# A hybrid encoder layer on one core: retention parts stored side by side, a written order for two more units of the projections, a new order at the retention's start, and unread products at the attention's end

## The chip, the core and the metric

The kernel runs on one core of a Trainium2 chip. The metric is the device time of one execution in microseconds (us). The kernel before took 1525.36 us, the median of three runs (1524.49 to 1526.89).

## The reference, cut to what matters

One layer, 1024 tokens of 1024 channels, all in float32:

```
h = RMSNorm(x); proj = h @ w_in                  # columns: aq ak av | rq rk rv rg
attn = dilated window attention(aq, ak, av)      # 8 heads of 64, three windows mixed by softmax of their lse
ret  = silu(rg) * GroupNorm(retention both ways) # 4 heads, rq/rk of 64, rv of 128
x += concat(attn, ret) @ w_out
x += memory cross attention(RMSNorm(x), RMSNorm(mem))   # 4 heads, 256 memory slots
x += top-1 group, then top-2 SwiGLU experts(RMSNorm(x)) # 32 experts
```

Retention is the chunk-wise form: in each chunk scores = (q k^T) * decay, y = scores v, and y += (decayed q) state, with state a sum of (decayed k)^T v over the other chunks, once forward and once backward.

## The kernel before, in words

**Split products.** Every float32 matrix product with two large operands is made as three products of rounded parts (`mm3`, lines 120 to 122): high x high, low x high and high x low. ScalarE makes a high part (`split`, line 112, or line 116 with a scale), and VectorE or GpSimd the low part (line 113 or 117) from the source and the high part.

**Stages, in us from the span's start.** Input projections 0 to 299; attention 299 to 443; retention with the first half of the out-projection 443 to about 538; the out-projection's second half to 588; memory keys to 645; memory queries and scores per block of 128 tokens to 798; memory output and routing to 935; 32 experts to 1507; the last scatter to 1523.

**What sets the order.** A planner orders the instructions of each engine and places the waits, except inside `tc.manual_schedule()`, where each engine and queue gets its instructions in the order in which the program is written. Written order holds before for the first four units of the projections, the attention loop, the retention, the last memory block and the experts. An engine takes its instructions in order: one that waits holds up all behind it.

**Input projections** (the loop over `s_`, 48 units: six blocks of 512 columns, c = 0 to 5, with 8 units each). A unit is 24 products of 128x512 into one of five "mm" banks (`proj` and `projT`). `W.split(c + 1, i)` makes the next block's weights (`wih`, line 116, and `wil`, line 117). In block c = 3 (`unit_rqk`) the units j = 0 to 3 are retention queries: `chain()` splits the result (tile `spr`, stored to `rT_s` high and low by two transfers), multiplies it by two decay tables (`qd`, line 452) and splits each (`spqd`, four transfers of 128 KB to `qd_s`, lines 368 and 369). Units j = 4 to 7 are keys: `chain()` also copies the result (`kf`, line 448), and `tail()`, one unit later, turns `kf` by four transposes (`tkd`, line 466), scales them (`kd`, line 472) and splits them into two tiles `kt`, stored to `kd_s`. All these split tiles share the tag "sp", which has two slots: a new one can be written when the store of the one two before it has landed. Block c = 4 (`unit_rv`) does the retention's values and stores `rvt` to `rv_s` by four transfers a unit, issued from SyncE's queue (SP).

**Attention's end.** `plan(n, f, place)` hangs work on the steps n = 0 to 82 of the loop; `planned(n, 0)`, `(n, 1)` and `(n, 2)` run it at three places in a step. At the steps from 73 on the scores are all made, and TensorE has the last weighted sums (`oB`), the retention's first key-value sums (`kv`), and the expansions of the final factors (`RA`, `RB`, line 961), which VectorE multiplies in (`tA`, `tB`, line 962).

**Retention's start.** `wo_part` (lines 1172 and 1174) splits a quarter of w_out into `woh` (ScalarE) and returns a function that makes the low part `wol` (VectorE). Before, the four high parts are made together and ahead of `ret_scores(Hs[0], 0)` and `(.., 1)`. `ret_scores` forms `rs` (line 1094) in one of two "sc" banks, and VectorE multiplies by the decay (`w`, line 1096); `ret_low` makes `wh` and `wl` (lines 1098 and 1104). In the loop over 16 steps i, the low parts `wol` come at i = 0, 1, 2 (2: two of them); the first out-projection products (`out_a`, lines 120 to 122 as `po<-woh,mx`) come from i = 2 on, and need `mx`, the split of the attention's result.

**Last memory block.** With u = 7 the products `vw` = values x w_mo (line 1831's banks) run between the block's scores; `put()` splits a result into `VW`, `Wm.split` makes `wmh` and `wml`, and `m_softmax(u, c)` is one piece: maximum (lines 1584, 1585), two exponentials with sums on ScalarE (line 1588), reciprocal and product (lines 1590, 1591).

**Experts.** Of each expert e: `gate_up` (products `p`), `x_T` (turning the next expert's gathered tokens, `xt`, line 1695, split into `x`), `h_T` (turning the activation, `ht`, line 1733), `h_split`, and the down products. `xt` and `ht` share the two banks of "tr". Ahead of the loop six small VectorE instructions (`nblk`, `nbi`, `nxf`, `nxi`, lines 2198 to 2203) count the blocks of overfull experts, for use behind the loop.

Of the kernel before, what the change touches and what calls it, by code (L numbers as in the profile page):

```python
# [20 lines left out]
P = 128  # L21
S = 1024
# [24 lines left out]
def kernel(  # L47
# [159 lines left out]
    rT_s = [dram([512, S], F32, f"rT_s{i}") for i in range(2)]  # L207
    qd_s = [dram([512, S], F32, f"qd_s{i}") for i in range(2)]
# [110 lines left out]
    with ExitStack() as c1:  # L319
# [51 lines left out]
        def parts(tag, name):  # L371
            t = st.tile([P, 4, 2, P], F32R, tag=tag, name=name).rearrange("p a i c -> p (a i c)")
            return [t[:, 512 * i:512 * i + 512] for i in range(2)]

# [3 lines left out]
        qw = col_weight(qnw, 1, "qw")  # L378
        kw = col_weight(knw, 1, "kw")
# [33 lines left out]
        def side_by_side(name):  # L413

            return st.tile([P, 4, 2, P], F32R, tag="sp", name=name)
# [20 lines left out]
        def unit_rqk(c, j):  # L436
# [6 lines left out]
            def chain():  # L443
                h, l = parts("sp", f"spr{f}{half}_")
                split(h, l, ps)
                store2([t[f * P:f * P + P, hs] for t in rT_s], h, l)
# [3 lines left out]
                for d in range(2):  # L450
# [3 lines left out]
                    h, l = parts("sp", f"spqd{f}{half}{d}_")  # L454
                    split(h, l, qd, pool)
# [24 lines left out]
        def unit_rv(c, u):  # L480
            ps = bank("mm", 5, f"prv{u}")

            def chain():
# [11 lines left out]
                for t in range(4):  # L495
                    nc.sync.dma_start(rv_s[:, 32 * r:32 * r + 32, 4 * half + t].rearrange("h p c -> p h c"),
                                      vt[32 * t:32 * t + 32])
# [123 lines left out]
        tail = None  # L621
        for s_ in range(48):
            c, j = divmod(s_, 8)
# [19 lines left out]
            if s_ == 10:  # L643
                log_decays()
            if s_ == 17:
                attn_consts()
# [8 lines left out]
            if s_ == 36:  # L655
                ret_consts()
# [42 lines left out]
    def load_qk(H):  # L699
# [3 lines left out]
        for i in range(2):  # L703
            nc.sync.dma_start(H.KS[64 * i:64 * i + 64].bitcast(F32), rT_s[i][256 + 64 * hd:256 + 64 * hd + 64, :])
            for j in range(2):
                nc.sync.dma_start(H.QQ[i][64 * j:64 * j + 64].bitcast(F32), rT_s[i][64 * hd:64 * hd + 64, :])
# [65 lines left out]
    with ch, ExitStack() as c2:  # L772
# [243 lines left out]
        for hp in range(4):  # L1016
# [19 lines left out]
            plan(n + (32 if hp < 3 else 22), lambda hp=hp: finish(pairs[hp]))  # L1036
        plan(74, lambda: chunk_sum(Hs[1], 2))
# [31 lines left out]
    with c4:  # L1069
# [153 lines left out]
        with tc.manual_schedule():  # L1223
# [147 lines left out]
    with ExitStack() as c5:  # L1371
# [52 lines left out]
        with ExitStack() as c7:  # L1424
# [153 lines left out]
            def m_softmax(u, c):  # L1578
                sp = SP_.pop((u, c))
                if c == 0:  # L1580
                    PR[u] = sb_.tile([P, 4, NMEM], F32, tag="prob", bufs=1, name=f"prob{u}")
                prob = PR[u]
                mx = sm().tile([P, 2], F32, tag="mmx", name=f"mmx{u}{c}")
                dve.tensor_reduce(mx, sp.rearrange("p (h m) -> p h m", h=2), axis=AX, op=OP.max)
                dve.tensor_scalar(mx, mx, -1.0, None, op0=OP.mult)
                den = sm().tile([P, 2], F32, tag="mden", name=f"mden{u}{c}")
                for h in range(2):
                    act.activation(prob[:, 2 * c + h], sp[:, 256 * h:256 * h + 256], AF.Exp, bias=mx[:, h:h + 1],
                                   accum_out=den[:, h:h + 1])
                dve.reciprocal(den, den)  # L1590
# [788 lines left out]
```

## Time and profile before

| | us |
|---|---|
| runs | 1524.49, 1526.89, 1525.36; median 1525.36 |
| profiled execution, whole time | 1525.24 |
| its span | 1523.4 |
| TensorE busy | 1469.8 (96%) |
| VectorE busy | 1143.5 (75%) |
| ScalarE busy | 887.4 (58%) |
| GpSimd busy | 234.5 (15%) |
| mean granted TensorE clock | 0.985 |

The profiled execution is 0.12 us under the median, with 1.84 us around its span. TensorE is busy nearly throughout, so the time is its work plus its few idle stretches, and its work takes twice as long where the granted clock is 0.50.

### The profile page before, as it was taken

What the parts mean: (1) busy time and instruction counts of PE and PEld (TensorE: products, weight loads), DVE (VectorE), ACT (ScalarE), POOL (GpSimd) and SP (SyncE); (2) the same over time, 40 slices, a digit from 0 to 9 for tenths busy, and PEclk for the clock granted to TensorE, in tenths of its full rate; (3) what the DMA queues carried; (4) which work ended last, traced back from release to release, by engine and by line L of the source; (5) the groups of instructions that cost most, each with busy time, mean ns of one, the idle gap of its engine ahead of it and who ended that gap; (6) DMA issues with size and microseconds to landing.
All of it is one profiled execution on the core that took longest, in us unless ns stands there. A gap on an engine that the chain in (4) does not pass through costs nothing. (4 is left out here: it accounts for less than half of the span.)

```text
span 1523.4 us, 22386 instructions
## 1 busy us (share of the span) xinstructions
PE 1469.8 (96%) x7722; PEld 1173.2 (77%) x7722; DVE 1143.5 (75%) x2557; ACT 887.4 (58%) x1493; POOL 234.5 (15%) x203
## 2 busy tenths in 40 slices
PE   8999989999999999999999998999999999999995
PEld 7788878798988877888878886777777777776663
DVE  8865355287766675987685668899898899888894
ACT  6431233297862243734352325888888888887783
POOL 0000134234410000000000003222232222221111
PEclk9999999999989999999999999999999999999998
DMA  8446775778569874730236747999999999999992
GB/s 304 111 125 193 203 238 161 207 208 253 183 200 281 315 286 138 244 119 29 74 112 220 263 153 258 357 349 363 367 375 366 362 367 367 368 362 362 365 383 82
DMA packets 121045, 383.64 MB, mean 252 GB/s; under 512 B 16288, under 2 KB 49312, under 8 KB 94432
## 3 DMA queue, kind: packets, MB, share of 16 engines
q1 hardware_dynamic: 112960, 361.32, 67.9%
q0 software_dynamic: 7968, 20.86, 5.4%
q8 instruction: 62, 1.02, 0.3%
q14 instruction: 55, 0.45, 0.1%
HBM read 318.81 MB, written 71.70 MB: 256 GB/s over the span
## 5 line engine op out<-in xcount | busy, mean ns | idle before, releaser
L120 PE MATMUL p<-eh,x 128*96 128x512 f32 x384 | 152.9, 398 | 0.2 <-ACT x L112 0.2
L122 PE MATMUL p<-el,x 128*96 128x512 f32 x384 | 151.5, 395 | 0.0
L121 PE MATMUL p<-eh,x 128*96 128x512 f32 x384 | 151.0, 393 | 0.1
L1685 POOL DMA_INDIRECT xg<-h_s,idx x32 | 79.1, 2472 | 282.8 <-PE xt L1695 276.1
L113 DVE TENSOR_TENSOR el<-ews,eh 128x1024 fp32r<-128x1024 f32 x86 | 100.7, 1219 | 14.1 <-ACT eh L112 14.1
L112 ACT ACTIVATE eh<-ews 128x1024 fp32r<-128x1024 f32 x86 | 87.3, 1054 | 19.3 <-DMA ews<-in_w_down_dram 9.6
L113 DVE TENSOR_TENSOR el<-ex,eh 128x1024 fp32r<-128x1024 f32 x76 | 89.3, 1219 | 5.5 <-ACT eh L112 5.0
L112 ACT ACTIVATE eh<-ex 128x1024 fp32r<-128x1024 f32 x76 | 77.8, 1055 | 9.8 <-PE p L121 6.5
L122 PEld LDWEIGHTS p<-el,x 128*96 128x96 f32 x384 | 62.1, 162 | 26.6
L121 PEld LDWEIGHTS p<-eh,x 128*96 128x96 f32 x384 | 62.2, 162 | 25.3 <-DVE x L113 0.4
L120 PEld LDWEIGHTS p<-eh,x 128*96 128x96 f32 x384 | 62.1, 162 | 24.6 <-ACT x L112 0.4
L1771 POOL DMA_INDIRECT out_dram<-yo,idx x32 | 50.0, 1562 | 170.0 <-ACT yo L1770 165.5
L113 DVE TENSOR_TENSOR el<-wraws,eh 128x1024 fp32r<-128x1024 f32 x60 | 70.3, 1219 | 3.4 <-ACT eh L112 3.3
L112 ACT ACTIVATE eh<-wraws 128x1024 fp32r<-128x1024 f32 x60 | 60.3, 1053 | 5.4 <-PE p L121 2.2
L1770 ACT ACTIVATE yo<-py,lists 96x512 f32<-96x512 f32 x64 | 43.2, 684 | 27.5 <-PE py L122 27.3
L113 DVE TENSOR_TENSOR ehl<-ex,ehl 128x1024 fp32r<-128x1024 f32 x46 | 54.0, 1215 | 0.0
L120 PE MATMUL po<-woh,mx 128*128 128x512 f32 x128 | 52.3, 408 | 1.8 <-DVE xr L1199 1.7
L120 PE MATMUL y<-VW,pT 128*128 128x512 f32 x128 | 53.0, 414 | 0.0
L113 DVE TENSOR_TENSOR ehl<-ews,ehl 128x1024 fp32r<-128x1024 f32 x44 | 51.8, 1217 | 1.5 <-ACT ehl L112 1.2
L120 PE MATMUL py<-ehl,hm 128*96 128x512 f32 x128 | 52.3, 408 | 0.0
L120 PE MATMUL mq<-wqh,hh 128*128 128x512 f32 x128 | 51.1, 401 | 1.0 <-ACT hh L112 1.0
L120 PE MATMUL pq<-wih,hTh 128*128 128x512 f32 x128 | 52.0, 406 | 0.0
(843 smaller groups left out, 4466.7 us busy)
## 6 DMA issues: line engine op xcount, KB each, us to landing
ews<-in_w_down_dram SPq DMA_DIRECT2D x30, 1024.0 KB, 14.3
ex<-in_w_gate_dram SPq DMA_DIRECT2D x25, 1024.0 KB, 13.6
wraws<-in_w_up_dram SPq DMA_DIRECT2D x23, 1024.0 KB, 13.0
ews<-in_w_gate_dram SPq DMA_DIRECT2D x20, 1024.0 KB, 10.5
ex<-in_w_up_dram SPq DMA_DIRECT2D x19, 1024.0 KB, 13.6
ews<-in_w_up_dram SPq DMA_DIRECT2D x15, 1024.0 KB, 11.8
ex<-in_w_down_dram SPq DMA_DIRECT2D x15, 1024.0 KB, 12.6
wi<-in_w_in_dram SPq DMA_DIRECT2D x11, 1024.0 KB, 6.2
```

The lines of the kernel that those rows point to most:

```text
L112: act.activation(hi, src, AF.Copy)
L113: (lo_engine or dve).tensor_tensor(lo, src, hi.bitcast(F32), OP.subtract)
L120: pe.matmul(ps, ah, bh, start=first, stop=False, **kw)
L121: pe.matmul(ps, al, bh, start=False, stop=False, **kw)
L122: pe.matmul(ps, ah, bl, start=False, stop=last, **kw)
L1685: pool.indirect_dma_start(out=self.xg[0:self.ns], out_offset=None, in_=h3_s, in_offset=bass.IndirectOffsetOnAxis(ap=self.ix, axis=0), boun ...
L1770: act.activation(yo[0:ns, 512 * c:512 * c + 512], self.py[c][0:ns], AF.Identity, scale=self.gate)
L1771: pool.indirect_dma_start(out=out, out_offset=bass.IndirectOffsetOnAxis(ap=self.ix, axis=0), in_=yo[0:ns], in_offset=None, bounds_check=S ...
```

## The change

In block c = 3 both parts of a split lie in one scratch tensor and go out in one transfer of 512 KB; the "sp" tag gets three slots; the units s_ = 24 to 39 are in written order, with the tail of unit 30 ahead of the next block's weight splits; the `rv_s` stores alternate between SP and GpSimd's queue; the retention's constants are made at unit 13 instead of 36. At the attention's end eight products of 128x128 are added whose result nobody reads. At the retention's start the scores come ahead of the first w_out split, the others are spread, and one "mm" bank is taken first. In the last memory block the softmax is in three pieces with a weight split between. Among the experts the first `h_T` uses a "y" bank, and the six small instructions come behind expert 1's `h_split`.

```diff
-    rT_s = [dram([512, S], F32, f"rT_s{i}") for i in range(2)]
-    qd_s = [dram([512, S], F32, f"qd_s{i}") for i in range(2)]
+    rT_s = dram([512, 2, S], F32, "rT_s")
+    qd_s = dram([512, 2, S], F32, "qd_s")
...
+        def both(name):
+            t = st.tile([P, 4, 2, P], F32R, tag="sp", bufs=3, name=name).rearrange("p a i c -> p (a i c)")
+            return t.rearrange("p (i t) -> p i t", i=2)
...
-                h, l = parts("sp", f"spr{f}{half}_")
-                split(h, l, ps)
-                store2([t[f * P:f * P + P, hs] for t in rT_s], h, l)
+                hl = both(f"spr{f}{half}_")
+                split(hl[:, 0], hl[:, 1], ps)
+                nc.sync.dma_start(rT_s[f * P:f * P + P, :, hs], hl.bitcast(F32))
...
-                    for j in range(2):
-                        hh = 2 * rp + j
-                        rows = slice(64 * j, 64 * j + 64)
-                        store2([t[P * hh + 64 * d:P * hh + 64 * d + 64, hs] for t in qd_s], h[rows], l[rows])
+                    hl = both(f"spqd{f}{half}{d}_")
+                    split(hl[:, 0], hl[:, 1], qd, pool)
+                    r0_ = 2 * P * rp + P * d
+                    nc.sync.dma_start(qd_s[r0_:r0_ + P, :, hs], hl.bitcast(F32))
...
+                    (nc.sync, pool)[t % 2].dma_start(rv_s[...], vt[32 * t:32 * t + 32])
...
+            if s_ == 24:
+                by_hand = c1.enter_context(ExitStack())
+                by_hand.enter_context(tc.manual_schedule())
+            if s_ == 40:
+                by_hand.close()
...
             p_()
+            if j == 7 and c == 3:
+                tail()
+                tail = None
             if j == 7 and c < 5:
                 for i in range(4):
                     W.split(c + 1, i)
...
+            if s_ == 13:
+                ret_consts()
-            if s_ == 36:
-                ret_consts()
...
     def load_qd(H):
         for i in range(2):
-            nc.sync.dma_start(H.qd[i].bitcast(F32), qd_s[i][H.hd * P:H.hd * P + P, :])
+            for d in range(2):
+                r0_ = 2 * P * (H.hd // 2) + P * d + 64 * (H.hd % 2)
+                nc.sync.dma_start(H.qd[i][64 * d:64 * d + 64].bitcast(F32), qd_s[r0_:r0_ + 64, i])
...
+        spare = []
+        plan(73, lambda: spare.append(bank("sc", 2, "spare")), 0)
+        for n in range(73, 77):
+            plan(n, lambda: busy_pe(spare[0], 2), 1)
...
-            wol = [wo_part(0, k // 2, k % 2, ro[:, k].rearrange("p (j f) -> p j f", j=2)) for k in range(4)]
+            wol = []
+            def wo_high(k):
+                wol.append(wo_part(0, k // 2, k % 2, ro[:, k].rearrange("p (j f) -> p j f", j=2)))
+            bank("mm", 1, "po_first")
             ret_scores(Hs[0], 0)
             ret_scores(Hs[0], 1)
+            wo_high(0)
             ret_low(Hs[0], 0)
...
                     wol[k]()
+                if i == 0:
+                    wo_high(1)
...
                     mix_part(0, 0, MX.pop(("r", 0)))
+                    wo_high(2)
+                    wo_high(3)
...
-                m_softmax(u, 0)
                 vw(4)
                 put()
+                held = Later(dve)
+                m_max(u, 0)
+                Wm.split(1, 0, held)
+                m_exp(u, 0)
+                held.go(1)
                 vw(5)
+                m_weights(u, 0)
                 put()
-                Wm.split(1, 0)
...
-                m_softmax(u, 1)
+                m_max(u, 1)
+                Wm.split(1, 1, held)
+                m_exp(u, 1)
+                held.go(1)
                 put()
-                Wm.split(1, 1)
+                m_weights(u, 1)
...
-            dve.tensor_scalar(nblk, nblk, float(P - 1), None, op0=OP.add)
-        ...
...
-                B[e].h_T()
+                B[e].h_T("y" if e == 0 else "tr")
                 B[e].h_split()
+                if e == 1:
+                    dve.tensor_scalar(nblk, nblk, float(P - 1), None, op0=OP.add)
+                ...
```

`busy_pe(ps, n)` makes n products of the 128x128 identity with itself; `Later` collects VectorE instructions and `held.go(1)` issues one.

## Rows read from the trace of the kernel before

**Rows 1.** The profile page: busy us (share of the span) and instructions of each engine.
```profile
PE 1469.8 (96%) x7722; PEld 1173.2 (77%) x7722; DVE 1143.5 (75%) x2557; ACT 887.4 (58%) x1493; POOL 234.5 (15%) x203
```

**Rows 2.** Waits of PE over the span: who waits, for whom, us in total, times, longest.
```profile
PE ht L1733 <- DVE x L113: 5.3, 5, 2.4
...
PE tkd L466 <- ACT kf L448: 2.6, 2, 2.4
PE vw L120 <- DVE VW L113: 2.6, 2, 1.3
...
PE prv L120 <- DVE qd L452: 1.4, 1, 1.4
...
PE po L122 <- DVE wol L1174: 1.1, 1, 1.1
```

**Rows 3.** Stretches of the span: start:end, length, busy us (and instructions) of PE, PEld, DVE, ACT and POOL, granted clock, DMA share, GB/s.
```profile
80.00:100.00 20.00, 20.00 (x95) 16.57 (x94) 13.58 (x51) 3.95 (x7) 0.00 (x0) 1.00 0.41 124
200.00:220.00 20.00, 16.23 (x74) 12.78 (x73) 14.77 (x27) 10.32 (x17) 5.85 (x9) 1.00 0.77 210
240.00:300.00 60.00, 60.00 (x264) 48.88 (x263) 17.44 (x28) 15.62 (x26) 18.10 (x34) 1.00 0.62 171
940.00:960.00 20.00, 17.59 (x85) 12.42 (x84) 18.68 (x25) 16.74 (x20) 2.48 (x2) 1.00 0.80 292
1000.00:1020.00 20.00, 20.00 (x95) 14.21 (x95) 18.23 (x20) 16.74 (x20) 5.84 (x3) 1.00 1.00 355
```

**Rows 4.** The chain of block c = 3: ScalarE in order of time (start, us, instruction, in brackets the idle time before it and what ended it).
```profile
185.46 0.60 ACT L112 ACTIVATE spr__1902<-prqk 128x512 fp32r<-128x512 f32 x1 [6.65 <-DMA qd_s<-spqd__1861]
...
194.43 0.60 ACT L112 ACTIVATE spr__1950<-prqk 128x512 fp32r<-128x512 f32 x1 [4.63 <-DMA qd_s<-spqd__1909]
...
200.00 2.74 ACT L116 ACTIVATE wih<-wi,mixw_t 128x512 fp32r<-128x512 f32 x4 [1.20 <-PE prqk L122]
...
216.09 0.60 ACT L448 ACTIVATE kf<-prqk 128x512 f32<-128x512 f32 x1 [1.37 <-DVE spr__2079 L113]
216.59 0.63 ACT L112 ACTIVATE kt<-kd 128x512 fp32r<-128x512 f32 x1
```

**Rows 5.** Transfers issued between 160 and 300 us, the group of 512 KB stores: tile, queue, count, KB each, median us from issue to landing.
```profile
kd_s<-kt SPq DMA_DIRECT2D x8, 512.0 KB, 3.0
```

**Rows 6.** The transposes of a key unit on PE, and VectorE's scaling of them, in order of time.
```profile
213.64 0.66 PE L466 MATMUL tkd<-ident,kf 128*128 128x128 f32 x4 [2.42 <-ACT kf L448]
...
214.33 1.13 DVE L472 TENSOR_SCALAR kd<-tkd,Gk 128x128 f32<-128x128 f32 x4 [1.38 <-PE tkd L466]
```

**Rows 7.** Stretches around idle time and clock changes, columns as in rows 3.
```profile
4.50:8.10 3.60, 0.01 (x1) 0.00 (x1) 2.14 (x11) 1.60 (x3) 0.00 (x0) 0.93 0.92 324
8.00:14.00 6.00, 5.90 (x17) 4.56 (x18) 5.41 (x13) 5.38 (x10) 0.00 (x0) 0.50 1.04 406
211.20:216.00 4.80, 2.38 (x14) 2.02 (x14) 3.22 (x9) 1.79 (x3) 0.00 (x0) 1.00 0.96 257
432.00:436.00 4.00, 3.29 (x26) 2.72 (x23) 2.29 (x7) 4.00 (x14) 0.00 (x0) 1.00 0.78 246
441.00:444.40 3.40, 3.09 (x21) 2.50 (x21) 1.41 (x3) 1.50 (x4) 0.00 (x0) 1.00 1.02 208
444.50:458.10 13.60, 12.40 (x49) 10.87 (x49) 9.91 (x17) 7.29 (x11) 0.57 (x1) 0.50 0.95 289
594.80:598.00 3.20, 3.20 (x9) 2.44 (x8) 2.76 (x8) 0.60 (x1) 0.00 (x0) 0.50 0.00 0
598.20:601.40 3.20, 3.20 (x16) 2.64 (x15) 0.00 (x0) 0.00 (x0) 0.00 (x0) 1.00 0.00 0
```

**Rows 8.** The retention's start in order of time, on ACT, DVE and PE.
```profile
448.36 3.88 ACT L1172 ACTIVATE woh<-ro 128x1024 fp32r<-128x1024 f32 x4
...
447.47 0.95 DVE L974 TENSOR_TENSOR tB<-tA,tB 128x768 f32<-128x768 f32 x1
...
454.01 0.68 DVE L1104 TENSOR_TENSOR wl<-w,wh 128x512 fp32r<-128x512 f32 x1
454.61 1.22 DVE L1174 TENSOR_TENSOR wol<-ro,woh 128x1024 fp32r<-128x1024 f32 x1
455.74 0.69 DVE L1096 SCALAR_TENSOR_TENSOR w<-rs,Dt_r 128x512 f32<-128x512 f32 x1
...
458.69 0.50 PE L121 MATMUL po<-woh,mx 128*128 128x512 f32 x1 [0.33 <-DVE mx L113]
```

**Rows 9.** The last memory block, DVE and PE in order of time.
```profile
779.20 0.17 DVE L1590 RECIPROCAL mden<-mden 128x2 f32<-128x2 f32 x1 [1.14 <-ACT prob L1588]
...
784.97 0.17 DVE L1590 RECIPROCAL mden<-mden 128x2 f32<-128x2 f32 x1 [1.15 <-ACT prob L1588]
...
786.52 0.50 PE L120 MATMUL vw<-wmh,vT 128*128 128x512 f32 x1 [1.30 <-DVE VW L113]
```

**Rows 10.** The first expert: DVE and PE in order of time.
```profile
941.34 0.17 DVE L2198 TENSOR_SCALAR nblk<-nblk 128x32 f32<-128x32 f32 x1
...
942.50 4.63 DVE L113 TENSOR_TENSOR el<-wraws,eh 128x1024 fp32r<-128x1024 f32 x4
...
949.92 1.01 DVE L113 TENSOR_TENSOR x<-xt,x 128x384 fp32r<-128x384 f32 x2
...
950.51 0.55 PE L1733 MATMUL ht<-ident,sg 96*128 96x96 f32 x4 [2.41 <-DVE x L113]
```

More of the change, by code (lines that the diff above doesn't have):

```diff
@@ L371, in parts @@
         def parts(tag, name):
-            t = st.tile([P, 4, 2, P], F32R, tag=tag, name=name).rearrange("p a i c -> p (a i c)")
+            t = st.tile([P, 4, 2, P], F32R, tag=tag, bufs=3, name=name).rearrange("p a i c -> p (a i c)")
             return [t[:, 512 * i:512 * i + 512] for i in range(2)]
+        def both(name):
+            t = st.tile([P, 4, 2, P], F32R, tag="sp", bufs=3, name=name).rearrange("p a i c -> p (a i c)")
+            return t.rearrange("p (i t) -> p i t", i=2)
         xts = {}
@@ L377 @@
         mixw_t = col_weight(mixw, KD, "mixw_t")
-        qw = col_weight(qnw, 1, "qw")
-        kw = col_weight(knw, 1, "kw")
+        qkw = consts.tile([P, 2], F32, name="qkw")
+        qw, kw = qkw[:, 0:1], qkw[:, 1:2]
+        nc.sync.dma_start(qw, qnw)
+        nc.sync.dma_start(kw, knw)
         W = Weights(w_in, whl, "wi", mixw_t)
@@ L413, in side_by_side @@
         def side_by_side(name):
-            return st.tile([P, 4, 2, P], F32R, tag="sp", name=name)
+            return st.tile([P, 4, 2, P], F32R, tag="sp", bufs=3, name=name)
         def unit_v(c, u):
@@ L495, in chain @@
                 for t in range(4):
-                    nc.sync.dma_start(rv_s[:, 32 * r:32 * r + 32, 4 * half + t].rearrange("h p c -> p h c"),
-                                      vt[32 * t:32 * t + 32])
+                    (nc.sync, pool)[t % 2].dma_start(rv_s[:, 32 * r:32 * r + 32, 4 * half + t].rearrange("h p c -> p h c"),
+                                                     vt[32 * t:32 * t + 32])
             return lambda: proj(ps, u, W.w[c]), chain, None
@@ L703, in load_qk @@
         for i in range(2):
-            nc.sync.dma_start(H.KS[64 * i:64 * i + 64].bitcast(F32), rT_s[i][256 + 64 * hd:256 + 64 * hd + 64, :])
+            nc.sync.dma_start(H.KS[64 * i:64 * i + 64].bitcast(F32), rT_s[256 + 64 * hd:256 + 64 * hd + 64, i])
             for j in range(2):
-                nc.sync.dma_start(H.QQ[i][64 * j:64 * j + 64].bitcast(F32), rT_s[i][64 * hd:64 * hd + 64, :])
+                nc.sync.dma_start(H.QQ[i][64 * j:64 * j + 64].bitcast(F32), rT_s[64 * hd:64 * hd + 64, i])
     def load_qd(H):
@@ L1576, in m_scores, with m_max, m_exp @@
                             dk == 0, dk == 1)
-            def m_softmax(u, c):
-                sp = SP_.pop((u, c))
+            def m_max(u, c):
                 if c == 0:
                     PR[u] = sb_.tile([P, 4, NMEM], F32, tag="prob", bufs=1, name=f"prob{u}")
-                prob = PR[u]
                 mx = sm().tile([P, 2], F32, tag="mmx", name=f"mmx{u}{c}")
-                dve.tensor_reduce(mx, sp.rearrange("p (h m) -> p h m", h=2), axis=AX, op=OP.max)
+                dve.tensor_reduce(mx, SP_[u, c].rearrange("p (h m) -> p h m", h=2), axis=AX, op=OP.max)
                 dve.tensor_scalar(mx, mx, -1.0, None, op0=OP.mult)
-                den = sm().tile([P, 2], F32, tag="mden", name=f"mden{u}{c}")
+                SP_["m", u, c] = mx
+            def m_exp(u, c):
+                sp, mx, prob = SP_.pop((u, c)), SP_.pop(("m", u, c)), PR[u]
+                den = SP_["d", u, c] = sm().tile([P, 2], F32, tag="mden", name=f"mden{u}{c}")
                 for h in range(2):
@@ L1594, in m_softmax @@
                     nc.sync.dma_start(prob_s[u * P:u * P + P, :], PR.pop(u).rearrange("p h m -> p (h m)"))
+            def m_softmax(u, c):
+                m_max(u, c)
+                m_exp(u, c)
+                m_weights(u, c)
             q_feat(0, tb)
@@ L1727, in swiglu, with h_T @@
                     dve.tensor_tensor(sv, sv, u, OP.mult)
-                def h_T(self):
+                def h_T(self, tag="tr"):
                     ns = self.ns
-                    self.hb = bank("tr", 2, f"ht{self.n}")
+                    self.hb = bank(tag, 2, f"ht{self.n}")
                     for i in range(4):
@@ L2197 @@
                 raws.free(B[0].raw(i), pool)
-            dve.tensor_scalar(nblk, nblk, float(P - 1), None, op0=OP.add)
-            dve.tensor_copy(nbi, nblk)
-            dve.tensor_scalar(nbi, nbi, 7, None, op0=OP.logical_shift_right)
-            dve.tensor_copy(nblk, nbi)
-            dve.tensor_reduce(nxf, nblk, axis=AX, op=OP.add)
-            dve.tensor_copy(nxi, nxf)
             for e in range(NEXP - 1):
@@ L2223 @@
                     B[e - 1].put()
-                B[e].h_T()
+                B[e].h_T("y" if e == 0 else "tr")
                 B[e].h_split()
+                if e == 1:
+                    dve.tensor_scalar(nblk, nblk, float(P - 1), None, op0=OP.add)
+                    dve.tensor_copy(nbi, nblk)
+                    dve.tensor_scalar(nbi, nbi, 7, None, op0=OP.logical_shift_right)
+                    dve.tensor_copy(nblk, nbi)
+                    dve.tensor_reduce(nxf, nblk, axis=AX, op=OP.add)
+                    dve.tensor_copy(nxi, nxf)
             e = NEXP - 1
```

5 lines of the change are left out of this document (3 added, 2 removed).

## The prediction

> **What bounds the kernel now.** I read the page first: TensorE is busy 96% of the span and no other engine comes near [rows 1]. The time is therefore TensorE's work at the granted clock, plus its idle stretches, and a change that adds or removes no large product can gain only idle time or half-rate time. So the next view was the list of TensorE's waits [rows 2]; the reader is to see that it is short, that no wait in it is over a few us in sum, and that most of its lines name an instruction that this change moves: the transposes of the retention keys, a value product behind `qd`, the products of values and w_mo, an out-projection product behind `wol`, and the experts' `ht`. Then came the stretches around these places [rows 3], for which engine is free to take what is moved in, and for the clock [rows 7], and at last each place in order of time, engine by engine.
>
> **Part A, the projections.** Before, TensorE idles 1.4 us ahead of a value product and 2.6 us ahead of two transposes [rows 2], 4.0 in all, which is the idle time of its stretch (16.23 busy of 20 [rows 3], the rest small). The row behind them is ScalarE's: a `spr` split waits 6.65 us for the store of an earlier `spqd` [rows 4]. The slots of "sp" make the chain late, and the transposes come when the chain lets them. After, three slots take the three tiles of a unit, and one 512 KB store replaces four issues. Such a store lands in 3.0 us by its nearest kin [rows 5]. A unit on TensorE is 24 products; 264 products take 60.00 us [rows 3], so 0.227 each and 5.5 a unit. A slot is held for the split (0.6 [rows 4]), the low part and the 3.0 of the store; that leaves 1.9 for a low part and its issue before the slots hold a unit up, so the chain just keeps pace. I take it that the 4.0 go.
>
> In written order something comes back. At unit 31 the tail of unit 30 stands between the products and the next weights. Its transposes are behind all 24 products of unit 31. From their start the first `kd` starts 0.69 later (214.33 against 213.64) and takes 1.13 [rows 6], the second takes as long again, to 2.9; `kt` takes 0.63, and the first `wih` 2.74/4 = 0.7 [rows 4], to 4.2. TensorE, whose transposes fill 0.66 [rows 6], has nothing else until then: 3.5 us idle. Before, this `wih` was made at 200.00 [rows 4], beside products, for the planner put it ahead. Bounds: 0, if a chain in hand lets ScalarE turn to the weights earlier, to 4.2. I take 3.5.
>
> Idle time has a second price. After 3.6 us without products (4.50 to 8.10) the granted clock was 0.50 in the stretch behind [rows 7]; around an idle 2.4 us (211.20 to 216.00) it stayed at 1.00 [rows 7]. 3.5 is nearest to the first, so I charge one half-rate stretch: 3.2 us of it do 9 products where 3.2 at full rate do 16 [rows 7], at half speed a loss of 1.6. Part A: -4.0 + 3.5 + 1.6 = **+1.1**, between -4.0 and +1.8.
>
> The rest of A I cost at nothing. The `rv_s` stores that go to GpSimd's queue fall where TensorE is busy 60.00 of 60 and GpSimd 18.10 [rows 3]; if GpSimd were late, its low parts of `rvt` would be, and nobody reads those before the retention. The constants moved to unit 13 are GpSimd work, two exponentials of ScalarE, in a stretch with GpSimd idle and TensorE full [rows 3]. `load_qd` issues four transfers instead of two a head, on SP, behind the loads of the attention's result, whose order is kept.
>
> **Part B and C, attention's end and retention's start.** From 444.50 to 458.10 the granted clock is 0.50, and TensorE is busy 12.40 of 13.60 [rows 7]: at full rate this is 6.2 us of work. The eight spare products lie in 432 to 441, where TensorE has some idle time (3.29 of 4.00 busy [rows 7]). A 128x128 transpose, the nearest row, costs 0.66/4 = 0.17 [rows 6], eight 1.3 at most; they fill gaps, so I cost them at 0. If the clock holds, VectorE bounds the stretch. Its instructions from `tB` on come in a line: `wl`, `wol` and `w` start at 454.01, 454.61 and 455.74 [rows 8], so 0.60 for a `wl` or `w` and 1.13 for a `wol`. `tB`'s add would end at about 447.75, when its earlier products run at full rate (448.42 before [rows 8]). Then come four `w`, three `wl`, two `wol` and 0.8 of `mx`, as written: 4.2 + 2.3 + 0.8 = 7.2, to 455.0. The new order is what lets them come without a gap, as 3.88 us of `woh` [rows 8] no longer stand ahead of the first `wh`. The mixed product of 458.69 [rows 8] comes at 455.0: -3.7. But 10.6 us with 6.2 of work leave TensorE 4.4 idle in pieces, the last of them long, so I charge one half-rate stretch here too: **-2.1**, between 0 and -3.7. The wait of 1.1 for `wol` [rows 2] stays: two `wol` still follow each other at i = 2, and their high parts now come later.
>
> A rule speaks against the spare products. What the rows show: in the 3.40 us before the fall TensorE was busy 3.09 [rows 7], with no idle stretch near those of part A. The Trainium skill, page "TensorE: Matmul & The Clock Gate", section "Why this matters for your kernels", has it that what costs the clock in the middle of a kernel are idle gaps of some length between bursts. By it the spare products would hold nothing, and B would be worth 0; the row differs from the rule, since the clock fell without such a gap. That case is the second rival.
>
> **Part D, last memory block.** TensorE waits 2.6 us, twice 1.3, for VectorE's `VW` [rows 2]. VectorE itself had waited 1.14 and 1.15 for the exponentials ahead of the reciprocals [rows 9]. The low part of `wm` (1.2 us, as other low parts of 1024 columns: 4.63/4 [rows 10]) now stands in these holes, and what follows moves up by the hole: 2.29 at most. I take **-2.3**; if only one wait goes, -1.0. ScalarE makes the high part ahead of the exponentials, while VectorE makes the maximum, so these are hardly later.
>
> **Part E, experts.** TensorE waits 2.41 for the first `ht`, whose bank `xt` held until `x` was split at 950.93 [rows 10]. In a "y" bank it waits for nothing but `sg`, and the six small instructions (941.34 to 942.50 [rows 10]) leave VectorE's line: everything behind them is 1.16 earlier. `x` then ends at 949.77 instead of 950.93, and the products that need its low part follow: **-1.5**, between -0.5 and -1.7. The six come behind expert 1, where TensorE is full; in such a stretch VectorE is busy 18.23 of 20 [rows 3], so they cost at most their 1.16 if that cover is gone.
>
> **Sum.** +1.1 - 2.1 - 2.3 - 1.5 = -4.8, against the profiled execution's 1525.24: 1520.4. That execution is 0.12 under the median of the runs, so the forecast stands for it as well. Less than about 0.2% (3 us) can't be told from no change.
>
> **Rivals.**
> 1. *The seam of unit 31 costs nothing.* The chain is so much in hand that weights and tail overlap, and no clock falls. For it: 4.0 idle are gone and VectorE has time. Against: one written order, and transposes behind the products. 1520.4 - 3.5 - 1.6 = 1515.3.
> 2. *Little comes through.* The clock falls at 444.5 all the same (spare products sit before 441, the fall comes later, and the clock fell with 3.09 of 3.40 busy [rows 7]); the new order alone gains about 1.1 there. And the experts are held by their weights: the DMA share is 1.00 [rows 3], so E's 1.5 is taken back. 1520.4 + 1.0 + 1.5 = 1522.9. Against the second half: the share is 0.80 at the place of E [rows 3], and a load starts when its slot is freed, so an earlier start is passed on.
> 3. *Slower: written order makes TensorE wait for the chain.* Before, the planner let the next block go on while the key chain was late: the value block's weights were made at 200.00, the `kf` of the second key unit at 216.09 [rows 4]. In written order every transpose, and the first `wih` behind the tail, waits for the chain. It decides when the lateness of eight units exceeds the 5.5 of slack that one unit gives: 0.7 a unit, a store of 3.7 us in place of 3.0. Price: at the pace of before, two query units' `spr` 9.0 apart (185.46 and 194.43 [rows 4]), 3.5 a unit are lost; four query units 14, less 5.5, is 8.5 and gives 1528.9; with key units as slow 14 more, 1542.9. I take the middle, 1536. Against it: 3.0 us for a store of this size [rows 5]; for it: written order gives no way around.
>
> **Chances.** Forecast, with its own range 1518 to 1522: 0.50. Rival 1: 0.15. Rival 2: 0.22, two thirds of it within 3 us of before. Rival 3: 0.13, nearly all of it slower. So faster by over 0.2%: 0.50 + 0.15 + 0.06 = 0.71; within: 0.17; slower: 0.12. The range holds forecast, rivals 1 and 2 and the near end of rival 3, 1515.0 to 1525.5; outside are most of rival 3 and some tails.
>
> **What would show it.** A right: no ScalarE wait of several us for `qd_s` or `rT_s`, `tkd` right behind products, and one idle stretch of about 3.5 us ahead of the first `prv`, with a clock of 0.50 behind it. B right: no 0.50 from 444.5. C right: the first mixed product about 11 us after `RB` starts. D: the two waits `vw` for `VW` gone. E: `ht`'s longest wait under 1 us. The prediction would be wrong if the transposes wait for `kf` again and again (rival 3), or if the gains are there until 935 and gone at the end (rival 2).

## The result and the profile after

The changed kernel took **1535.82 us**, the median of six runs (1532.10 to 1541.63), beside 1525.04 for the kernel before in the same runs (1521.34 to 1526.99). The ratio is 1.0066 with a 95% interval of 1.0047 to 1.0085: slower by some 10 us, where 1520.4 was forecast, in a range up to 1525.5. The profiled execution took 1537.01 with a span of 1535.2, 11.8 more than before.

The changed kernel's waits of PE, to be laid beside [rows 2]:

```profile
PE kv L120 <- DMA v_r<-rv_s: 4.2, 1, 4.2
...
PE prv L120 <- ACT wih L116: 3.6, 1, 3.6
...
PE oB L906 <- ACT phB L112: 3.3, 1, 3.3
PE ht L1776 <- DVE x L113: 3.2, 4, 1.1
...
PE vw L120 <- DVE VW L113: 1.2, 2, 0.7
```

Every wait that the prediction named for going is gone or shorter: the two for the late chain (`tkd`, `prv` behind `qd`) are not in the list, `vw` went from 2.6 to 1.2, and `ht` from 5.3 to 3.2 with a longest of 1.1. The predicted new one is there (`prv` behind `wih`, 3.6). But two large waits are there that the prediction doesn't know: 3.3 for `phB`, in the middle of the attention, and 4.2 for a load of `v_r`, in the retention. Around these places the change touches little but loads.

Stretches of the changed kernel around the three idle places and at the attention's end (columns as in [rows 3]; the DMA share is the mean busy share of the sixteen DMA engines, so 1.00 means all are busy):

```profile
205.20:208.90 3.70, 0.05 (x2) 0.01 (x1) 2.18 (x9) 1.93 (x4) 1.62 (x2) 0.81 0.42 166
208.90:214.30 5.40, 5.14 (x11) 3.65 (x12) 5.40 (x8) 4.72 (x8) 0.87 (x1) 0.50 0.48 194
365.60:369.00 3.40, 0.15 (x3) 0.03 (x1) 0.05 (x1) 1.16 (x3) 2.84 (x2) 0.84 1.03 230
369.00:378.20 9.20, 9.20 (x43) 9.20 (x44) 4.96 (x18) 6.05 (x20) 5.87 (x5) 0.50 0.29 94
443.00:453.20 10.20, 10.15 (x84) 9.61 (x85) 5.10 (x16) 3.17 (x8) 0.24 (x1) 1.00 1.03 303
453.20:456.60 3.40, 3.17 (x15) 2.88 (x15) 3.27 (x6) 1.58 (x3) 0.57 (x1) 0.51 1.03 258
...
463.50:466.90 3.40, 3.40 (x11) 2.83 (x10) 0.58 (x1) 0.00 (x0) 0.00 (x0) 0.50 1.07 246
509.00:514.00 5.00, 0.83 (x8) 0.65 (x7) 3.03 (x11) 1.32 (x3) 0.00 (x0) 1.00 1.03 215
514.70:518.10 3.40, 3.40 (x16) 3.24 (x16) 0.51 (x2) 0.00 (x0) 0.00 (x0) 0.50 1.02 354
```

Each idle stretch is followed by one at a granted clock of 0.50: 5.4 us of it behind the seam, 9.2 behind `phB` (all of it with PE fully busy, so about 4.6 us of work lost), 3.4 behind `v_r`. So each of the two unknown waits costs more than its idle time. At both the DMA share is 1.03 and the transfers bring 215 to 230 GB/s.

What stands behind `phB`, changed kernel in order of time on POOL, ACT and PE:

```profile
359.27 1.04 POOL L308 CAST QA<-QB 128x1024 fp32r<-128x1024 f32 x1 [17.48 <-PE sB L837]
...
365.48 2.33 POOL L988 TENSOR_TENSOR tB<-tA,tB 128x1024 f32<-128x1024 f32 x1
...
367.84 0.59 ACT L913 ACTIVATE tB<-oB 64x512 f32<-64x512 f32 x1 [6.19 <-POOL tB L988]
...
368.97 1.22 PE L906 MATMUL oB<-phB,vB 128*128 128x256 f32 x4 [3.25 <-ACT phB L112]
```

Read from the bottom: TensorE waits for ScalarE, which waited 6.19 us for GpSimd's `tB`; GpSimd ran without a pause from 359.27, and began only then, with the conversion of a loaded tile (`QB`). The engine named in its bracket (`PE sB`) had long been done; the experiments below show that it is the load. So one load that lands late, at 359, ends as an idle TensorE at 366.

To see where the 11.8 us arise, the trace of each kernel was cut at the same products (first or last start or end on TensorE), and the length of each piece taken, in us. "tail" is the changed kernel with the tail moved back (below), "half rows" and "half columns" are the kernel before with another load of `qd` (below):

```
piece (from .. to)                       before  changed  tail    half rows  half columns
projections, rqk to the end              140.13  141.97   135.62  141.04     141.05
attention, to its last score             115.43  120.79   119.83  118.76     115.11
to the last RB                            31.60   31.00    31.00   30.92      30.91
to the first mixed product                11.26    8.50     8.52   11.06      11.05
retention, to its last kv                 53.86   61.22    57.68   60.83      52.64
to the memory tokens' first transpose     78.73   80.81    80.79   80.34      78.73
to the first vw                          176.37  174.57   174.62  174.75     176.35
last memory block                         31.24   29.28    29.59   31.26      31.23
to the first expert's products           137.91  140.45   139.63  139.10     138.15
first expert's products to the last p    559.78  558.25   557.85  562.19     558.25
```

Against before, the changed kernel loses 1.8 in the projections, 5.4 in the attention, 7.4 in the retention, 2.1 behind it and 2.5 at the routing; it gains 0.6 and 2.8 at the retention's start, 1.8 ahead of `vw` (a half-rate stretch of before, [rows 7] at 594.80, isn't there), 2.0 in the memory block and 1.5 among the experts. With 0.3 less ahead of the first piece this makes 10.2, and from the last product `p` to the end it is 1.5 more.

Each column is a single execution, and not all of these differences are the change's. In the kernels of the experiments that leave a stage as it was, the projections take 139.5 to 141.7 us and the way to the first `vw` 174.6 to 176.7, with the half-rate stretch near 594 in some and not in others; the piece to the first expert's products takes 138.2 to 141.1 in all other kernels, so that before's 137.91 is the shortest of them (3.4 us at half rate there, 10.2 in the changed kernel from 941.4 on). And the 1.5 at the end stand in every kernel on the changed projections: from the start of the last scatter to the end of the span it is 15.3 to 16.5 us in them and 13.7 to 14.1 in those on the projections of before. What it is there no run shows. The losses in the attention and the retention are beyond this spread.

### The profile page after: what moved, and what is told of

Its sections match the earlier page's. It is cut to its first block, busy times and chain, and to the rows that moved or that the text cites. A ratio compares the mean times of both kernels' runs of the same rounds, so it can differ in the third digit from the quotient of the medians.

```text
span 1535.2 us, 22354 instructions
## 1 busy us (share of the span) xinstructions
PE 1472.6 (96%) x7738; PEld 1176.9 (77%) x7738; DVE 1144.3 (75%) x2557; ACT 889.3 (58%) x1493; POOL 241.8 (16%) x219
## 5 line engine op out<-in xcount | busy, mean ns | idle before, releaser
L113 DVE TENSOR_TENSOR el<-ews,eh 128x1024 fp32r<-128x1024 f32 x86 | 100.7, 1218 | 15.3 <-ACT eh L112 13.2
L112 ACT ACTIVATE eh<-ex 128x1024 fp32r<-128x1024 f32 x76 | 78.0, 1059 | 10.5 <-PE p L121 5.2
L1814 POOL DMA_INDIRECT out_dram<-yo,idx x32 | 51.3, 1603 | 169.4 <-ACT yo L1813 164.8
L122 PE MATMUL po<-wol,mx 128*128 128x512 f32 x128 | 51.3, 401 | 1.0 <-DVE wol L1196 1.0
L1221 DVE TENSOR_TENSOR xr<-po,xr 128x512 f32<-128x512 f32 x32 | 22.1, 690 | 40.4 <-PE po L122 40.3
```

The costliest lines, as they stand in the source:

```text
L112: act.activation(hi, src, AF.Copy)
L113: (lo_engine or dve).tensor_tensor(lo, src, hi.bitcast(F32), OP.subtract)
L122: pe.matmul(ps, ah, bl, start=False, stop=last, **kw)
L1221: return lambda: dve.tensor_tensor(XO[u][:, cc], ps, XO[u][:, cc], OP.add)
L1814: pool.indirect_dma_start(out=out, out_offset=bass.IndirectOffsetOnAxis(ap=self.ix, axis=0), in_=yo[0:ns], in_offset=None, bounds_check=S ...
```

## The experiments

All times are medians of up to 12 runs beside runs of the kernel before on the same chip (1526.68 to 1527.48 there, so compare by the ratio to before); "1.0038 [1.0018, 1.0058]" is a ratio with its 95% interval. The profile of each kernel is one execution. The quoted texts were written before the runs; their theories H, N and S are named in the first.

**The load of qd in halves, alone (half rows).** The kernel before, with only this:

```diff
-            nc.sync.dma_start(H.qd[i].bitcast(F32), qd_s[i][H.hd * P:H.hd * P + P, :])
+            for d in range(2):
+                r0_ = H.hd * P + 64 * d
+                nc.sync.dma_start(H.qd[i][64 * d:64 * d + 64].bitcast(F32), qd_s[i][r0_:r0_ + 64, :])
```

> The kernel before, with one thing of the change: each load of qd in two transfers of 64 rows. Theory H (transfers of 64 rows slow the queue that all loads of the attention and the retention share, so later loads land late): the two stalls that the changed kernel has beside the predicted ones, 3.3 us for phB in the attention's second part and 4.2 us for v_r in the retention, come with their half-rate stretches, +5 to +11 us, 1530 to 1536. Theory N (it is the number of transfers): the same here. Theory S (the stalls come from something else in the change, the written order or the stores): within 2 us of before, 1525.

1538.53 us, 1.0071 [1.0051, 1.0091]: +11, as much as the whole change. Theory S falls.

**As many transfers, all rows in each (half columns).**

```diff
+                cs = slice(512 * d, 512 * d + 512)
+                nc.sync.dma_start(H.qd[i][:, cs].bitcast(F32), qd_s[i][H.hd * P:H.hd * P + P, cs])
```

> The kernel before, with each load of qd in two transfers of 128 rows and half the columns: as many transfers as in the changed kernel, all rows in each. Theory H: within 2 us of before, 1525. Theory N: as the kernel with half the rows, 1530 to 1536. Theory S: 1525.

1527.21 us, 1.0000 [0.9989, 1.0011]: nothing. It is the rows, not the number. The two kernels are twins up to the load, so the same stretch can be compared, first half rows (the order of the loads on SP, two stretches, the start of GpSimd's conversion, and the waits of PE):

```profile
336.05 3.86 SPq L713 DMA_DIRECT2D qd_r<-qd_s  x4
...
342.90 4.50 SPq L269 DMA_DIRECT2D QB<-qT_s  x2
...
342.00:346.00 4.00, 3.85 (x31) 3.42 (x30) 2.38 (x12) 4.00 (x16) 0.00 (x0) 1.00 1.03 283
346.00:350.00 4.00, 4.00 (x33) 3.72 (x33) 3.96 (x11) 2.19 (x7) 0.00 (x0) 1.00 1.03 252
...
358.87 1.04 POOL L308 CAST QA<-QB 128x1024 fp32r<-128x1024 f32 x1 [17.72 <-DMA QB<-qT_s]
...
PE kv L120 <- DMA v_r<-rv_s: 4.7, 1, 4.7
...
PE oB L890 <- ACT phB L112: 3.5, 1, 3.5
```

and half columns:

```profile
342.00:346.00 4.00, 3.85 (x31) 3.41 (x29) 2.38 (x11) 4.00 (x16) 0.00 (x0) 1.00 1.03 393
346.00:350.00 4.00, 4.00 (x33) 3.72 (x33) 3.97 (x12) 2.19 (x7) 0.00 (x0) 1.00 1.01 407
...
356.02 1.04 POOL L308 CAST QA<-QB 128x1024 fp32r<-128x1024 f32 x1 [14.91 <-DMA QB<-qT_s]
...
PE oB L890 <- ACT phB L112: 0.7, 1, 0.7
...
PE kv L120 <- DMA v_r<-rv_s: 0.2, 1, 0.2
```

The DMA engines are busy in both (1.01 to 1.03), but move 283 and 252 GB/s instead of 393 and 407. `QB`, queued behind, is converted 2.9 us later, and the two waits of the changed kernel come up, 3.5 and 4.7 for 0.7 and 0.2. Theory H holds, and N falls.

**One transfer of 128 rows from the new scratch tensor.** The changed kernel, the source written as two groups of 64 rows:

```diff
-            for d in range(2):
-                r0_ = 2 * P * (H.hd // 2) + P * d + 64 * (H.hd % 2)
-                nc.sync.dma_start(H.qd[i][64 * d:64 * d + 64].bitcast(F32), qd_s[r0_:r0_ + 64, i])
+            src = qd_s.rearrange("(r d j x) i t -> r j i d x t", r=2, d=2, j=2)[H.hd // 2, H.hd % 2, i]
+            nc.sync.dma_start(H.qd[i].bitcast(F32), src)
```

> The changed kernel with each part of qd loaded by one transfer of 128 rows again, gathered from the two places of the new scratch tensor. Theories H and N: both unpredicted stalls go and their half-rate stretches with them, -9 to -11 us against the changed kernel, 1525 to 1527. Theory S: they stay, 1536.

1596.48 us, 1.0456 [1.0436, 1.0475]: the theories missed it by 60 to 70 us. Stretches of this kernel:

```profile
345.00:350.00 5.00, 5.00 (x40) 4.60 (x40) 4.09 (x12) 3.19 (x11) 0.00 (x0) 1.00 0.13 50
...
365.00:368.00 3.00, 0.00 (x0) 0.00 (x0) 0.00 (x0) 0.00 (x0) 0.00 (x0) 0.50 0.13 53
...
492.00:495.00 3.00, 0.00 (x0) 0.00 (x0) 0.00 (x0) 0.00 (x0) 0.00 (x0) 1.00 0.13 53
```

A share of 0.13 is two of sixteen engines, at 50 to 53 GB/s: the transfer whose outermost dimension is 2 was carried by two engines, and all else queued behind it; whole microseconds pass with every engine idle. **The same with the tail behind the splits:**

> As the one before, and the tail of unit 30 behind the next block's weight splits again, as in all other blocks. Theories H and N: the idle 3.65 us ahead of the first value product go to under 1 us and the half-rate stretch behind it goes, -4 to -5 more, about 1521. Theory S: -4 to -5 against the changed kernel, 1531. If the tail is not what holds the weights up, the idle time stays and it is as the kernel before it.

1587.80 us, 1.0401 [1.0381, 1.0421]: 8.7 less for the tail (4 to 5 expected), though beside such stalls the size says little.

**Rows in the order of the heads.** The changed kernel, with loads of 128 successive rows and, for it, stores of 64:

```diff
-                    r0_ = 2 * P * rp + P * d
-                    nc.sync.dma_start(qd_s[r0_:r0_ + P, :, hs], hl.bitcast(F32))
+                    for j in range(2):
+                        r0_ = P * (2 * rp + j) + 64 * d
+                        nc.sync.dma_start(qd_s[r0_:r0_ + 64, :, hs], hl[64 * j:64 * j + 64].bitcast(F32))
...
+            nc.sync.dma_start(H.qd[i].bitcast(F32), qd_s[H.hd * P:H.hd * P + P, i])
```

> The changed kernel with the rows of qd_s in the order of the heads: a store goes out in two transfers of 64 rows (in place of one of 128), and a load is one transfer of 128 successive rows. Theory H (64-row loads are what makes later loads late): the waits for phB in the attention and for v_r in the retention go, -9 to -11 us against the changed kernel, 1525 to 1528. If the price lies in the new scratch tensor itself (its rows 8 KB apart), they stay, 1536.

1531.91 us, 1.0038 [1.0018, 1.0058], which is 4 us less against before than the changed kernel and not 9 to 11. The wait for `v_r` went and that for `phB` fell to 0.5, though the scratch tensor's rows are as far apart as in the changed kernel; but the chain is late now. Waits of PE:

```profile
PE tkd L472 <- ACT kf L455: 4.1, 1, 4.1
...
PE prv L120 <- ACT wih L116: 3.6, 1, 3.6
```

This is rival 3's mechanism, transposes that wait for a late chain: the projections take 147.77 us here instead of 141.97. With one store more per tile the chain no longer keeps pace.

**The tail moved back**, first in the changed kernel, then in the kernel with the heads' rows (which the second text below calls the one before):

```diff
-            if j == 7 and c == 3:
-                tail()
-                tail = None
```

> The changed kernel with one thing undone: the tail of unit 30 stands behind the next block's weight splits again. If the seam costs what the prediction says (3.5 idle, 1.6 of half rate), -5 us against the changed kernel, about 1533; the waits for phB and v_r stay. If two kernels that differed by the tail alone (1531.9 and 1522.8) show its price, -9, about 1529.

1530.01 us, 1.0023 [1.0010, 1.0037], some 6.6 less than the changed kernel by the ratios (1.0066 - 1.0023). The wait for `wih` is gone, and `phB` and `v_r` stay:

```profile
PE oB L903 <- ACT phB L112: 3.7, 1, 3.7
...
PE kv L120 <- DMA v_r<-rv_s: 2.1, 1, 2.1
```

> As the one before, with the tail of unit 30 behind the next block's weight splits. If that tail holds up the weights, as the prediction has it, the 3.65 us idle ahead of the first value product go, and the half-rate stretch behind it: -4 to -5 us, 1520 to 1523. If the chain is the limit anyway, no difference.

1522.78 us, 0.9977 [0.9963, 0.9991]: 9 less than with the tail ahead (4 to 5 expected), and faster than before. Against the changed kernel with its tail moved back (1.0023) the loads of 128 rows are worth 7 us here, though a wait of 3.1 for `kf` is left in its trace.

**One of the two stores from GpSimd's queue**, `(nc.sync, pool)[j].dma_start(...)` in the kernel just above:

> The changed kernel with rows in the order of the heads (loads of 128 rows), the tail behind the weight splits, and of the two stores of a tile one from SyncE's queue and one from GpSimd's. If SyncE's queue (two issues of 0.6 us in line) makes the slots late, the remaining 3.1 us wait of the transposes for kf goes, and it is 3 us under the kernel with both on SyncE, about 1520. If a slot is held by the transfer itself, no difference, 1523.

1526.42 us, 0.9997 [0.9984, 1.0010]: no gain; if anything 3 us are lost against the kernel just above. Its longest wait of `tkd` for `kf` is 4.5, so taking one issue off SyncE doesn't free the slots earlier; whether the transfer holds them, or GpSimd's own work the second issue, isn't shown.

**Attention's end and retention's start, alone**: with everything, without the unread products, and without the bank taken first.

> The kernel before with the attention's end and the retention's start of the change alone. By the prediction -2.1: the clock holds through 444.5 and the first mixed product comes 3.7 us earlier, with one half-rate stretch given back. Of the changed kernel's trace: -3.3 at the first mixed product, -2.0 by the second head, and +1.8 from a new wait for xr at the out-projection's second half, if that wait comes from the bank taken first: then about 0, 1525 to 1527.

1526.43 us, 0.9997 [0.9985, 1.0008]: no gain that can be told from nothing. The -2.1 of the prediction (0.9986) lies at the edge of the interval.

> The kernel before with the retention's start alone, without the unread products. If the products hold the clock, the half-rate time around 444.5 is as before (10 to 13.6 us) and this kernel is about 1.5 us slower than the one with them (with them 6.8 us of half rate). If they hold nothing (the second rival), both have the same half-rate time and the same total.

1525.57 us, 0.9989 [0.9976, 1.0002], the same without the products.

Stretches of the kernel without the products, and then of the one with them:

```profile
444.90:448.30 3.40, 3.40 (x16) 3.17 (x16) 3.21 (x6) 1.39 (x3) 0.57 (x1) 0.50 1.02 252
...
455.20:458.60 3.40, 3.40 (x11) 2.73 (x10) 0.51 (x1) 0.00 (x0) 0.00 (x0) 0.50 1.05 212
```

```profile
446.30:453.10 6.80, 6.80 (x32) 6.57 (x32) 6.46 (x12) 4.27 (x6) 0.57 (x1) 0.50 1.06 289
```

Both have 6.8 us at half rate, the one in two pieces, the other in one; the kernel before has 13.6 [rows 7]. In this pair the products hold nothing that can be seen, and the new order without them has half the half-rate time. Two kernels further down also have the new order without the products, and their traces differ; `b_best` (the first that is built of what the runs favour) and then `a_best2` (the second):

```profile
449.40:452.70 3.30, 3.30 (x16) 3.08 (x15) 2.86 (x8) 1.87 (x3) 0.57 (x1) 0.50 1.07 275
```

```profile
443.40:453.50 10.10, 9.41 (x41) 8.88 (x42) 7.55 (x14) 4.27 (x6) 0.57 (x1) 0.50 1.05 321
```

So there are 3.4, 6.8 and 10.2 us at half rate without the products, 3.4 to 6.8 in the seven traces with them (the two kernels with stalls of two engines left out), and 10.2 to 13.7 with the old order. That the order shortens the half rate is likely; what the products add is not settled by so few executions, and no time shows a gain. The rule of the Trainium skill that the prediction weighed against them (page "TensorE: Matmul & The Clock Gate", section "Why this matters for your kernels") would have had them worthless; the pair of traces above agrees, the three together don't decide it.

```diff
-            bank("mm", 1, "po_first")
```

> The kernel before with the attention's end and the retention's start of the change, without the line that takes an mm bank first. If that line moves the banks so that the out-projection's second half waits 1.8 us for xr, this wait goes here, and 0.7 us for kv ahead of the first scores comes back: -1 against the kernel with the line, about 1525. If the bank has nothing to do with it, the 1.8 stay.

1523.86 us, 0.9979 [0.9967, 0.9992]. The wait of the out-projection's second half, with the line and without:

```profile
PE po L120 <- DVE xr L1203: 3.5, 3, 1.8
```

```profile
PE po L120 <- DVE xr L1203: 1.7, 2, 1.4
```

One wait of 1.8 comes and goes with the line, as expected, and the piece behind the retention goes from 80.81 to 78.71. The wait of 0.7 for `kv` ahead of the first scores came back, as expected too; by the ratios the line costs 2.7 (0.9997 - 0.9979) where 1 was expected. Why it makes the wait isn't shown: no run tells which banks lie where.

**Softmax and experts**, together and each alone:

> The kernel before with the softmax in pieces and the experts' start of the change alone. By the prediction -2.3 and -1.5, together -3.8, 1523 against 1527 in the same job. Rival (the experts' weights take it back): the memory block is 2 us earlier, and the end is at the time of before.

1522.83 us, 0.9967 [0.9951, 0.9983]: -5.0 for the expected -3.8.

> The kernel before with the softmax in pieces alone. Prediction: -2.3, with the vw waits for VW going from 2.6 to under 0.5; of the changed kernel's trace: -2.0, waits 1.2.

1527.25 us, 1.0005 [0.9994, 1.0015]. The wait is shorter, though not under the expected 0.5, and the block with it (29.46 us instead of 31.24), but the runs as a whole show no gain:

```profile
PE xt L1705 <- DMA xg<-h_s,idx: 1.9, 1, 1.9
...
PE vw L120 <- DVE VW L113: 1.1, 2, 0.7
```

> The kernel before with the experts' start alone. Prediction: -1.5, with the first wait of ht under 0.5. Rival (the weights of the experts give the end): the first ht earlier by 1.5, the end as before.

1525.32 us, 0.9995 [0.9985, 1.0005]. The first `ht` on PE in its trace, which waited 2.41 before [rows 10], now waits for `sg` alone:

```profile
955.27 0.55 PE L1733 MATMUL ht<-ident,sg 96*128 96x96 f32 x4 [0.33 <-DVE sg L1727]
```

The two alone come to nothing in sum (1.0005 and 0.9995), where the two together gave 0.9967; they ran in other sessions, and the traces don't show where the difference lies. They do show what the experts' start does. From the first product `p` to the second scatter of an expert's output it is 51.3 to 53.1 us in the seven traces without it and 49.8 to 51.3 in the eleven with it. Four of the seven have a half-rate stretch behind the first `ht` that none of the eleven has, such as this one (the kernel of the attention's end and the retention's start):

```profile
950.49 0.55 PE L1748 MATMUL ht<-ident,sg 96*128 96x96 f32 x4 [1.79 <-DVE x L113]
...
951.60:954.80 3.20, 3.20 (x9) 2.11 (x8) 2.81 (x3) 2.80 (x3) 0.00 (x0) 0.50 0.90 309
```

**Everything that the runs favour.** First on the projections of before (retention's start without the bank, softmax, experts):

> The kernel before with the retention's start (without the bank taken first), the softmax in pieces and the experts' start; the projections, the qd loads and the attention as before. If the parts add up, -3.2 (measured with the unread products) and -4.7: about -8, 1519.5 against 1527.5 in the same session, and under both kernels. If the gains take each other's place (the weights of the experts give the end), -4.

1521.32 us, 0.9975 [0.9962, 0.9988]: -3.8, so the parts do not add up to the expected -8.

And on the projections of the change (heads' rows, tail back, no bank, no products):

> The changed kernel with qd_s in the order of the heads, the tail behind the weight splits, no bank taken first and no unread products: every part of the change in a form that the runs favour. If the projections in written order are worth something without their two prices, 2 to 4 us under b_best, 1516 to 1518; if the chain at the limit takes it back (3.1 us wait of the transposes for kf), as b_best, 1519 to 1521.

1523.23 us, 0.9977 [0.9965, 0.9989], over both of the expected spans. Both beat both kernels, by 3.5 to 4 us under before; between them there is no difference that these intervals tell, so the projections in written order, in this form, earn nothing that can be measured.

## Why the prediction was wrong

**The step that failed** is one sentence of part A: "`load_qd` issues four transfers instead of two a head, on SP, behind the loads of the attention's result, whose order is kept", costed at nothing. It named a cover, but only for the head whose load stands there. The first head's load is issued in the attention, ahead of `QB`, and the third's and fourth's in the retention, right behind a `v_r`; each is in flight with loads that TensorE soon needs. And it counted transfers, where the number is free (half columns, 1.0000) and the rows are not (half rows, 1.0071). The term should have been +11 instead of 0; with it the sum is -4.8 + 11 = +6, and +8 with the 2.1 behind the retention that it also lacked. Measured were +10; the 1.5 at the end are a term that the sum lacks as well.

The rows to see it by were at hand in the trace of the kernel before. It loads 64 rows at a time elsewhere (`QQ_r`, `KS_r`); here is a stretch with these in flight, and then one with `qd_r` and `vB`, which have 128 rows:

```profile
334.00:338.00 4.00, 3.44 (x27) 3.24 (x28) 3.70 (x18) 3.93 (x14) 0.62 (x1) 1.00 1.05 228
...
342.00:346.00 4.00, 3.85 (x31) 3.34 (x30) 2.63 (x8) 4.00 (x15) 0.00 (x0) 1.00 1.03 413
```

The engines are as busy in both. The Trainium skill speaks of it too: the page "DMA: Bandwidth & Descriptors", section "Rules for kernel authors", says of two transfers to disjoint halves of the partitions not to bother, since both halves go over the same engines and so serialize, and to use one of 128 partitions. The runs agree and add the price: the engines busy at 1.03 in both kernels, and 252 to 283 GB/s for 393 to 407.

**The other terms, in their order.**
- *The chain's 4.0 us.* Right: with the tail moved back the projections take 135.62 us, 4.5 less than before, and 3.9 under the shortest of the kernels that leave them as they were.
- *The seam.* Right in place and mechanism: 3.65 idle for `wih` (3.5 forecast), and a half-rate stretch behind it. The size was a little low: 5.1 forecast, 6.4 between 141.97 and 135.62, as the half rate lasted longer. The two together came to +1.8 in this pair of executions, +1.1 forecast; that they are so near is partly luck, as the same projections of before take 139.5 to 141.7 in other traces.
- *Attention's end and retention's start.* The first mixed product comes 2.8 + 0.6 earlier by the pieces (3.7 forecast for that), but no run shows a gain from B, as the second rival had it. Where the part lost its gain is the line that takes a bank first, costed at nothing without a word: 1.8 for `xr`. In sum 0.9997 [0.9985, 1.0008] for -2.1 (which would be 0.9986). In the working, 4.2 + 2.3 + 0.8 is 7.3 and not 7.2, and 444.50 to 455.0 is 10.5; the -3.7 stands.
- *Softmax.* -2.0 in its piece (-1.8 alone), for -2.3.
- *Experts.* The first wait went from 2.41 [rows 10] to 0.33. That the experts' piece is 1.5 shorter, as forecast, is luck: 1.1 of it lies between the second scatter and the 22nd (353.1 us before, 352.0 in the changed kernel), where nothing was changed and the kernel with the experts' start alone takes 353.1 as well; 0.6 lies at the start. What the sum lacked is the half-rate stretch that the wait has behind it in four of seven traces. Softmax and experts together are worth 0.9967 [0.9951, 0.9983], -5 for -3.8.
- *What stays open.* The softmax alone shows its 1.8 in its piece and not in the total. In its profile the routing behind takes 3.1 us longer than before, with a wait of 1.9 for the first gather of tokens (1.3 in the changed kernel, 0.2 before) and 10.2 us at half rate where before has 3.4. As before has the shortest routing of all traces, this is no price of the softmax that could be named. Why the gather lands later in some executions, and why the parts do not add up, isn't shown.

**The rivals.** The time of rival 3, 1536, was met, but not by its mechanism: in the changed kernel no transpose waits for the chain. Its mechanism is real one step further on, as the kernel with stores of 64 rows shows.

## What to carry to other kernels

When a layout changes to save stores, price the loads as well: count the partitions of each new transfer, and look at what is queued behind it in a stage whose DMA share is near 1. Count for a wait that a change opens the half-rate stretch behind it too (here 3.3 idle and 9.2 us at half rate for `phB`). And a part that is costed at nothing for its cover needs that cover named for each place where it runs, not for one. Last, lay a piece of one trace beside the same piece of several kernels that leave it alone, before its difference is called the change's.

## What the runs showed of the hardware that had not been expected

- With transfers into 64 partitions in flight the DMA engines were as busy as with those into 128, at about two thirds of the rate (283 and 252 GB/s for 393 and 407). Full loads issued behind them landed later as well: `vB`, of 128 rows, 13.2 us after its issue with half rows and 10.2 with half columns.
- A transfer whose source has an outermost dimension of 2 ran on two of the sixteen engines (share 0.13, 50 to 53 GB/s). The Trainium skill has the rule, page "DMA: Bandwidth & Descriptors", section "Rules for kernel authors": an outermost dimension under 16 confines a transfer to at most as many engines. The trace agrees.
- In the changed kernel a stretch at 0.50 stood behind each idle stretch of 3.3 to 4.2 us. But one also stood behind an idle 1.8 us (the first `ht` above), while the idle 2.4 us of [rows 7] had none, and one at the attention's end with TensorE busy 10.15 of 10.20 us right before. So the longest idle stretch alone doesn't tell when the clock falls.
